# Ending layer norms in one VectorE pass, and moving small transfers of attention to another queue

## The chip, the cores and the metric

The kernel runs on one core of a Trainium2 chip. Times are device microseconds of the whole program; the time of a kernel is the median of several runs. The engines are TensorE (PE, with its weight loads PEld), VectorE (DVE), ScalarE (ACT), GpSimd (POOL) and SyncE (SP), which here only issues transfers (DMAs). Each engine works through its own list in order.

## The reference

Two layers of a decoder trunk, 1024 positions of width 1024 in float32. Layer 0 mixes tokens by dilated sliding-window attention, layer 1 by a gated linear recurrence; each mixer is followed by an MLP with squared ReLU (width 4096). After each of the four sub-layers:

```python
x <- layer_norm(alpha * x + sublayer(x), g, b)     # alpha = 4 ** 0.25

def layer_norm(x, g, b):
    mu = mean(x); var = mean((x - mu) ** 2)
    return (x - mu) * rsqrt(var + 1e-5) * g + b
```

Attention has three head groups with (window, dilation) = (128, 1), (512, 4), (2048, 16) and 16 heads of 64 columns each. A group gives, per position and head, an output and the logarithm of its softmax denominator (from the row maximum m and the sum l of exponentials); the three outputs are mixed with weights softmax(lse) over the groups, and the mix goes through the output matrix.

## The kernel before

Matrices are split in a high and a low part, and each product is three matmuls, so TensorE has most of the work. The input products of attention and the MLP's products follow a scheme that uses seven half-sized products in place of eight.

The work of attention is cut in 24 units: a pair of heads (8) by a group, in the order of dilation 16, 4, 1 within a pair. The units lie between the input products: `at(slot, f)` puts a step of a unit behind a certain product, with the slots written out by hand (`STATS`, `MIX`, `OFFS`). Through the body of attention the order of TensorE and VectorE is fixed as written (`in_order`); elsewhere, and on the other engines, a planner orders the instructions by the program's order and its own estimate of when they can start.

A unit's steps: `qk` (scores, with row maximum and exponential; the statistics go to `allS`), `ptr` and `pv` (transposed weights times values), then `combine_tr`: TensorE transposes `allS` (L566), ScalarE copies 32 rows of it to `sr` (L569), SP stores them in DRAM (L572) and loads them again into `ml` with a row for 16 (head, block) pairs (L578 for dilation 1, L581 for the others, where positions are regrouped). When a pair's third unit is through, `combine` works out the three factors per position on VectorE and ScalarE (L595 to L614), splits them in `fh` and `fl`, and SP copies six times two rows into the tile `frow` (L619). In `combine_mul` TensorE spreads a row of `frow` over the partitions (`fb`, L629) and VectorE multiplies the output with it (L630), adds the groups (L632, L633) and stores the mix.

The last two units don't fit between input products. Their steps stand in the hand-written list `mine` and are worked off by `tick` between the matmuls of the output product (`outproj_ln`: weights `wor`, activations `onr`, residual `z`, all by SP, with splits by ScalarE and VectorE at L137 and L138). The tail of attention is this stretch, from about 960 to 1062 us.

Every norm goes through `ln_math`, in place on a tile `z` of 128 positions by 1024 columns: statistics (L196, L198), `(z - mean) * g` in one VectorE pass (L199), the reciprocal root by ScalarE's logarithm and exponential with one step of refinement in small VectorE instructions (L204 to L206). The last eight of 32 norms, with `store`, end in two half passes on VectorE (L210). The other 24 end so:

```python
act(z, z, AF.Copy, scale=w[:, 3:4])      # L213, ScalarE
nc.gpsimd.tensor_add(z, z, bB)           # L214, GpSimd
```

Then `z` is stored for the next residual (L996, L1300) and transposed on TensorE (`lnpt`, L223), whose results are split by ScalarE and VectorE (L233, L234). In `outproj_ln` the calls `fin(t)` and `tr(t)` interleave products, norms and transposes of the eight tiles; L991 and L993 empty a product's PSUM bank (three banks `mm`) into `z`. In `ffn` norms are spread by `todo` between the steps of the second product.

Of the kernel before, what the change touches and what calls it, by code (L numbers as in the profile page):

```python
# [9 lines left out]
F32 = mybir.dt.float32  # L10
F32R = mybir.dt.float32r
U8 = mybir.dt.uint8
AF = mybir.ActivationFunctionType
ALU = mybir.AluOpType
AX = mybir.AxisListType

P = 128
# [5 lines left out]
DIL = (1, 4, 16)  # L23
# [39 lines left out]
def trunk_kernel(  # L63
# [24 lines left out]
    nc = tc.nc  # L88
# [7 lines left out]
    def U(name, dt=F32):  # L96
        return up.tile([P, 1024], dt, name=name, tag="u")

    def bank(tag, name):
        return ps.tile([P, 512], F32, name=name, tag=tag, bufs={"mm": 3, "s": 2, "pt": 2, "o": 1}[tag])  # L100

    def small(shape, name, bufs=4, dt=F32):
        return sp.tile(shape, dt, name=name, tag=name, bufs=bufs)

    act = nc.scalar.activation
# [87 lines left out]
    def ln_math(z, gB, bB, store=None):  # L193
        st = small([P, 2, 6], "lnst")
        for i in range(2):
            nc.vector.bn_stats(st[:, i], z[:, i * 512:(i + 1) * 512])  # L196
        mv = small([P, 2], "lnmv")
        nc.vector.bn_aggr(mv, st)  # L198
        nc.vector.scalar_tensor_tensor(z, z, mv[:, 0:1], gB, op0=ALU.subtract, op1=ALU.mult)  # L199
        w = small([P, 4], "lnw")  # L200
        act(w[:, 0:1], mv[:, 1:2], AF.Ln, bias=eps_ln)
        act(w[:, 1:2], w[:, 0:1], AF.Exp, scale=-0.5)
        r = w[:, 1:2]
        nc.vector.tensor_scalar(w[:, 2:3], mv[:, 1:2], LN_EPS, r, op0=ALU.add, op1=ALU.mult)  # L204
        nc.vector.tensor_scalar(w[:, 2:3], w[:, 2:3], r, -0.5, op0=ALU.mult, op1=ALU.mult)
        nc.vector.tensor_scalar(w[:, 3:4], w[:, 2:3], 1.5, r, op0=ALU.add, op1=ALU.mult)  # L206
        if store is not None:
            for i in range(2):
                c = slice(i * 512, i * 512 + 512)
                nc.vector.scalar_tensor_tensor(z[:, c], z[:, c], w[:, 3:4], bB[:, c], op0=ALU.mult, op1=ALU.add)  # L210
                nc.sync.dma_start(store[:, c], z[:, c])
            return
        act(z, z, AF.Copy, scale=w[:, 3:4])  # L213
        nc.gpsimd.tensor_add(z, z, bB)  # L214

    def z_tr(z):

# [104 lines left out]
    def attention(pre, hc):  # L322
# [121 lines left out]
        frow = U("frow", F32R)  # L444
# [19 lines left out]
        def nat(ap, g):  # L464
            d = DIL[g]
            return ap if d == 1 else ap.rearrange("p (n r) -> p n r", r=d)
# [97 lines left out]
        def combine_tr(pr, g, slot, ml):  # L564
            pt = bank("pt", "mpt")
            nc.tensor.transpose(pt[:, 0:P], allS, ident)  # L566
            q = slice(slot * 32, slot * 32 + 32)
            sr = small([P, P], "sr", 2)
            act(sr[q], pt[q, 0:P], AF.Copy)  # L569
            yield  # L570
            md = mdram[pr, g]
            nc.sync.dma_start(md.rearrange("w h (b q) -> (w h b) q", q=P), sr[q])  # L572
            yield

            d = DIL[g]
            for w in range(2):
                if d == 1:
                    nc.sync.dma_start(ml[:, w, 0, :], md[w].rearrange("h (i n) -> (h i) n", n=P))  # L578
                else:
                    for h in range(2):  # L580
                        nc.sync.dma_start(  # L581
                            ml[8 * h:8 * h + 8, w, g, :].rearrange("i (r n) -> i r n", r=d),
                            md[w, h].rearrange("(r i n) -> i r n", r=d, i=8))
            yield

        def combine(pr, ml):
            def cv(tl, g):
                d = DIL[g]
                return tl if d == 1 else tl.rearrange("p (r n) -> p n r", r=d)

            m = ml[:, 0]
            l = ml[:, 1]
            v = nc.vector
            mn = small([16, P], "mn", 1)
            v.tensor_tensor(nat(mn, 1), nat(m[:, 0], 1), cv(m[:, 1], 1), op=ALU.min)  # L595
            v.tensor_tensor(nat(mn, 2), nat(mn, 2), cv(m[:, 2], 2), op=ALU.min)
            for g in range(NG):
                v.tensor_sub(cv(m[:, g], g), nat(mn, g), cv(m[:, g], g))
            act(m, m, AF.Exp)
            yield  # L600
            v.tensor_mul(l, l, m)
            den = mn
            v.tensor_add(nat(den, 1), nat(l[:, 0], 1), cv(l[:, 1], 1))
            v.tensor_add(nat(den, 2), nat(den, 2), cv(l[:, 2], 2))
            yield
            v.reciprocal(den, den)
            for g in range(NG):
                v.tensor_mul(nat(l[:, g], g), cv(m[:, g], g), nat(den, g))

            fh = wp.tile([P, 512], F32R, name="fh", tag="p")[:16, :NG * P].rearrange("p (g t) -> p g t", t=P)  # L610
            fl = wp.tile([P, 512], F32R, name="fl", tag="pts")[:16, :NG * P].rearrange("p (g t) -> p g t", t=P)
            act(fh, l, AF.Copy)
            yield
            v.tensor_sub(fl, l, fh.bitcast(F32))  # L614
            yield
            for g in range(NG):
                for i, f in enumerate((fh, fl)):
                    r = 4 * g + 2 * i
                    nc.sync.dma_start(frow[r:r + 2, :].bitcast(F32).rearrange("h (i t) -> h i t", t=P),  # L619
                                      f[:, g, :].bitcast(F32))  # L620
            yield

        def combine_mul(pr, og, hb):
# [26 lines left out]
        ml, ogs = {}, {}  # L650
# [58 lines left out]
        def unit_work(gi, a, base):  # L709
# [20 lines left out]
            work = []  # L730
            later = [lambda: [f() for f in work.pop(0)] for _ in range(5)]
            trs = combine_tr(pr, g, slot, ml[pr])
            stats = [lambda: next(trs, None)] * 3
            mix = []
            if g == GORD[-1]:
                steps = combine(pr, ml[pr])
                mix = [lambda: next(steps, None)] * 5
                for hb in range(2):
                    muls = combine_mul(pr, ogs[pr], hb)
                    mix += [lambda muls=muls: next(muls, None)] * (4 + hb)  # L740
# [24 lines left out]
        for n in range(len(seq)):  # L765
            gi, i, j = seq[n]
# [26 lines left out]
            if n % 21 == 14:  # L793
# [27 lines left out]
        (ra, ca, sa, _), (rb, cb, sb_, mx) = tail  # L821
        done = [f for n in sorted(fill) for f in fill[n]]
        mine = [[ra[0]], [rb[0], rb[1]], [ra[1]], [ca[0], rb[2]], [ca[1]], [cb[0]], [ca[2]], [cb[1]], [ca[3]], [cb[2]],
                [ca[4]] + sa, [cb[3]], [ca[5]], [cb[4]] + sb_, [cb[5]], mx[:1], mx[1:3], mx[3:5], [],
                mx[5:7], mx[7:10], mx[10:]]
        lists = [done[k:k + 1] + (mine[k] if k < len(mine) else []) for k in range(max(len(done), len(mine)))]
        return oN, lists
# [62 lines left out]
    def outproj_ln(pr, oN, fill, resid, gB_ap, bB_ap, keep):  # L890
# [92 lines left out]
        def fin(t, dms=(0, 1)):  # L983
            load_z(t)
            for dm in dms:
                o = bank("mm", "pmm")
                c = slice(dm * 512, dm * 512 + 512)
                old = parts.get((t, dm), [])
                rows(o, a, w, t, dm, [k for k in range(NK) if k not in old], True, True)
                if old:  # L990
                    nc.vector.tensor_add(z[t][:, c], o, z[t][:, c])  # L991
                else:
                    nc.vector.scalar_tensor_tensor(z[t][:, c], z[t][:, c], ALPHA, o, op0=ALU.mult, op1=ALU.add)  # L993
            if 1 in dms:
                ln_math(z[t], gB, bB)
                nc.sync.dma_start(keep[t * P:(t + 1) * P, :], z[t])  # L996
# [22 lines left out]
    def ffn(li, xf, late, res, gB_ap, bB_ap, last, pre=None):  # L1019
# [275 lines left out]
        def norm_of(t):  # L1295
            if last:
                ln_math(z[t], norm["g"], norm["b"], out[t * P:(t + 1) * P, :])
                return
            ln_math(z[t], norm["g"], norm["b"])
            nc.sync.dma_start(x3d[t * P:(t + 1) * P, :], z[t])  # L1300
# [188 lines left out]
    def hgrn(xs, late, consts, pre, gw):  # L1489
# [104 lines left out]
        for hd in range(8):  # L1594
# [66 lines left out]
            if hd == 0:  # L1661
                new = [[]] + new
            pend = [(pend[i] if i < len(pend) else []) + (new[i] if i < len(new) else [])
                    for i in range(max(len(new), len(pend)))]
# [9 lines left out]
    pr = Out(w_attn_out, "a", 0)  # L1674
    hc = []
    oN, fill = attention(pr.pre_steps, hc)
    xf, late = outproj_ln(pr, oN, fill, lambda t: x[t * P:(t + 1) * P, :],
                          ln_mix_g[0], ln_mix_b[0], x1d)
# [85 lines left out]
```

## Time and profile before

| | us |
|---|---|
| median of 3 runs | 2829.61 (2828.23 to 2829.97) |
| profiled execution, its own time | 2828.98 |
| span of the profile | 2827.2 |
| TensorE busy / VectorE / ScalarE / GpSimd | 2766.7 / 2069.0 / 1450.8 / 122.9 |

The profile lists instructions by source line with engine, output and inputs, e.g. `L214 POOL TENSOR_TENSOR z<-z,bB`. In the timeline a row begins with its start and its duration; a bracket says how long the engine was idle before and what released it. A wait row reads "who waits <- for whom: us in total, times, longest". A group row of one source line gives the least, the median and the greatest duration in ns. "SPq" is SP's queue of transfers: its durations are those of issuing, not of the transfer. PEclk is the share of TensorE's full clock that was granted.

### The profile page before, as it was taken

The numbers are of one execution on the slowest core, as the hardware profiler recorded it, in microseconds if no ns is written. First come the engines' busy times: TensorE is split into PE (matmuls) and PEld (weight loads), VectorE is DVE, ScalarE is ACT, GpSimd is POOL, SyncE is SP. The second block draws the span as 40 slices with busy tenths as digits, with TensorE's granted clock in tenths as the row PEclk, the third lists the DMA queues.
The fourth block names the chain that finished last, engine by engine and source line by source line (L and its number), as shares of the span: only waits on it lengthen the run. The fifth ranks groups of instructions, "written<-read, shape, count | busy, mean of one in ns | idle before, by whom it ended". The sixth has DMA issues, their size and how long they took to land.

```text
span 2827.2 us, 40131 instructions
## 1 busy us (share of the span) xinstructions
PE 2766.7 (98%) x14280; PEld 2229.3 (79%) x14280; DVE 2069.0 (73%) x3830; ACT 1450.8 (51%) x3105; POOL 122.9 (4%) x68
## 2 busy tenths in 40 slices
PE   8999999999999989999999999999999999999998
PEld 6777777777777757888878887788887788878887
DVE  7768777777877767786686876565667787678687
ACT  5455555655555555544454444555553644454443
POOL 0000000000000003100000011111102200000000
PEclk9999999999999999999999999999999999999999
DMA  7766665766666523464494752011132355475654
GB/s 286 255 187 208 191 207 173 217 201 198 201 200 220 168 83 134 146 224 160 152 324 127 260 178 98 8 60 60 61 112 104 128 211 176 154 278 188 221 176 130
DMA packets 204936, 485.27 MB, mean 172 GB/s; under 512 B 29376, under 2 KB 43712, under 8 KB 204736
## 3 DMA queue, kind: packets, MB, share of 16 engines
q1 hardware_dynamic: 204736, 482.72, 51.1%
q8 instruction: 112, 1.84, 0.3%
q14 instruction: 88, 0.72, 0.1%
HBM read 362.82 MB, written 94.24 MB: 162 GB/s over the span
## 4 chain that ended last, share of the span: by engine, by line
PE 90%; DVE 5%; ACT 2%; DMA 1%; issue 1%; POOL 0%; SPq 0%; DVEq 0%; POOLq 0%; ACTq 0%
PE pmm L669 8%; PE pmm L671 8%; PE pmm L670 8%; PE pup L1118 7%; PE pup L1116 7%; PE pup L1117 7%; PE pdy L1268 4%; PE pdy L1264 4%; PE pdy L1267 4%; PE s L502 3%; PE pdx L1267 3%; PE pmm L171 3%; PE pdx L1268 3%; PE pmm L173 3%; PE pdx L1264 3%; PE pmm L172 3%
## 5 line engine op out<-in xcount | busy, mean ns | idle before, releaser
L669 PE MATMUL pmm<-xh,H 128*128 128x512 f32 x1008 | 408.5, 405 | 13.2 <-ACT H L432 9.6
L671 PE MATMUL pmm<-xh,H 128*128 128x512 f32 x1008 | 396.5, 393 | 0.2 <-DVE H L440 0.2
L670 PE MATMUL pmm<-xl,H 128*128 128x512 f32 x1008 | 396.0, 393 | 0.0
L669 PEld LDWEIGHTS pmm<-xh,H 128*128 128x128 f32 x1008 | 190.8, 189 | 54.1 <-ACT H L432 9.6
L671 PEld LDWEIGHTS pmm<-xh,H 128*128 128x128 f32 x1008 | 190.4, 189 | 42.6 <-DVE H L440 1.1
L670 PEld LDWEIGHTS pmm<-xl,H 128*128 128x128 f32 x1008 | 191.1, 190 | 36.6
L516 ACT ACTIVATE p<-p,stats 128x128 f32<-128x128 f32 (+1 forms) x384 | 168.3, 441 | 90.7 <-DVE stats L513 89.3
L1264 PE MATMUL pdy<-dT,dS 128*128 128x512 f32 x512 | 199.2, 389 | 0.0
L1267 PE MATMUL pdy<-dT,dS 128*128 128x512 f32 x512 | 199.2, 389 | 0.0
L1268 PE MATMUL pdy<-dT,dS 128*128 128x512 f32 x512 | 199.2, 389 | 0.0
L513 DVE CUSTOM_DVE_ANT_0 p<-s,mask 128x128 f32<-128x128 f32 (+1 forms) x384 | 113.3, 348 | 66.5 <-PE s L502 56.8
L137 ACT ACTIVATE dS<-dr 128x512 fp32r<-128x512 f32 x192 | 119.5, 622 | 73.1 <-PE pdy L1268 36.6
L171 PE MATMUL pmm<-f0nh,wh 128*128 128x512 f32 x384 | 153.1, 399 | 0.0
L173 PE MATMUL pmm<-f0nh,wl 128*128 128x512 f32 x384 | 150.1, 391 | 1.7 <-DVE wl L138 1.6
L172 PE MATMUL pmm<-f0nl,wh 128*128 128x512 f32 x384 | 149.8, 390 | 0.0
L138 DVE TENSOR_TENSOR dS<-dr,dS 128x512 fp32r<-128x512 f32 x192 | 135.4, 705 | 16.2 <-ACT dS L137 14.3
L214 POOL TENSOR_TENSOR z<-z,bB 128x1024 f32<-128x1024 f32 x24 | 58.6, 2444 | 1673.1 <-ACT z L213 1663.0
L529 ACT ACTIVATE pts<-ppt 128x256 f32<-128x256 f32 (+1 forms) x192 | 85.4, 474 | 61.1 <-PE ppt L526 59.0
L137 ACT ACTIVATE dT<-hold 128x512 fp32r<-128x512 f32 x128 | 80.0, 625 | 69.0 <-DVE hold L1243 28.4
L1077 ACT ACTIVATE H<-wc 128x512 fp32r<-128x512 f32 x128 | 77.2, 625 | 73.3 <-DVE wc L1070 43.9
L1267 PEld LDWEIGHTS pdy<-dT,dS 128*128 128x128 f32 x512 | 96.1, 188 | 20.0
L1268 PEld LDWEIGHTS pdy<-dT,dS 128*128 128x128 f32 x512 | 96.1, 188 | 20.0
(396 smaller groups left out, 6946.6 us busy)
## 6 DMA issues: line engine op xcount, KB each, us to landing
xh<-xtd SPq DMA_DIRECT2D x110, 512.0 KB
xl<-xtd SPq DMA_DIRECT2D x110, 512.0 KB
dr<-hd SPq DMA_DIRECT2D x192, 256.0 KB
dr<-in_w_down_dram SPq DMA_DIRECT2D x128, 256.0 KB
rot<-e SPq DMA_DIRECT2D x192, 128.0 KB
wa<-in_w_up_dram SPq DMA_DIRECT2D x48, 512.0 KB
wb<-in_w_attn_dram SPq DMA_DIRECT2D x36, 512.0 KB
wa<-in_w_attn_dram SPq DMA_DIRECT2D x33, 512.0 KB
```

The costliest lines, as they stand in the source:

```text
L137: act(hi, raw, AF.Copy)
L171: nc.tensor.matmul(o, wh[:, k], xs.h(k), start=k == 0, stop=False)
L172: nc.tensor.matmul(o, wh[:, k], xs.l(k), start=False, stop=False)
L173: nc.tensor.matmul(o, wl[:, k], xs.h(k), start=False, stop=k == NK - 1)
L669: nc.tensor.matmul(o, wh, hi[k // 2][:, c], start=begin and k == 0, stop=False, skip_group_check=True)
L670: nc.tensor.matmul(o, wh, lo[k // 2][:, c], start=False, stop=False, skip_group_check=True)
L671: nc.tensor.matmul(o, wl, hi[k // 2][:, c], start=False, stop=end and k == 3, skip_group_check=True)
L1116: nc.tensor.matmul(o, wh, xf.h(b, k), start=begin and k == 0, stop=False, skip_group_check=True)
L1117: nc.tensor.matmul(o, wh, xf.l(b, k), start=False, stop=False, skip_group_check=True)
L1264: nc.tensor.matmul(o[q], h, T_[:, L], start=begin, stop=False, skip_group_check=True)
L1267: nc.tensor.matmul(o[q], h, T_[:, R], start=False, stop=False, skip_group_check=True)
L1268: nc.tensor.matmul(o[q], l, T_[:, L], start=False, stop=end, skip_group_check=True)
```

## The change

`ln_math` without `store` ends in one VectorE instruction, z * factor + bias, in place of the ScalarE and the GpSimd instruction. In `combine_tr` the store of `sr` is issued by ScalarE; for dilation 1 there is no store and no load, but two copies from `sr` straight into `ml`, issued by ScalarE too. The loads for dilations 4 and 16 stay on SP. In `combine` the rows of `fh` are issued by ScalarE and those of `fl` by SP. In the list `mine` the first step of the statistics (transpose and copy) of the last unit moves ahead of the step `cb[4]`, the others ahead of `cb[5]`; for the unit before, the other steps move one place back.

```diff
-        act(z, z, AF.Copy, scale=w[:, 3:4])
-        nc.gpsimd.tensor_add(z, z, bB)
+        nc.vector.scalar_tensor_tensor(z, z, w[:, 3:4], bB, op0=ALU.mult, op1=ALU.add)
...
-            q = slice(slot * 32, slot * 32 + 32)
+            q0 = slot * 32
             sr = small([P, P], "sr", 2)
-            act(sr[q], pt[q, 0:P], AF.Copy)
+            act(sr[q0:q0 + 32], pt[q0:q0 + 32, 0:P], AF.Copy)
             yield
             md = mdram[pr, g]
-            nc.sync.dma_start(md.rearrange("w h (b q) -> (w h b) q", q=P), sr[q])
+            d = DIL[g]
+            if d == 1:
+                for w in range(2):
+                    nc.scalar.dma_start(ml[:, w, 0, :], sr[q0 + 16 * w:q0 + 16 * w + 16])
+            else:
+                nc.scalar.dma_start(md.rearrange("w h (b q) -> (w h b) q", q=P), sr[q0:q0 + 32])
             yield
-            d = DIL[g]
-            for w in range(2):
-                if d == 1:
-                    nc.sync.dma_start(ml[:, w, 0, :], md[w].rearrange("h (i n) -> (h i) n", n=P))
-                else:
+            if d > 1:
+                for w in range(2):
                     for h in range(2):
                         nc.sync.dma_start(
                             ml[8 * h:8 * h + 8, w, g, :].rearrange("i (r n) -> i r n", r=d),
...
-                for i, f in enumerate((fh, fl)):
+                for i, (f, eng) in enumerate(((fh, nc.scalar), (fl, nc.sync))):
                     r = 4 * g + 2 * i
-                    nc.sync.dma_start(frow[r:r + 2, :].bitcast(F32).rearrange("h (i t) -> h i t", t=P),
-                                      f[:, g, :].bitcast(F32))
+                    eng.dma_start(frow[r:r + 2, :].bitcast(F32).rearrange("h (i t) -> h i t", t=P),
+                                  f[:, g, :].bitcast(F32))
...
-                [ca[4]] + sa, [cb[3]], [ca[5]], [cb[4]] + sb_, [cb[5]], mx[:1], mx[1:3], mx[3:5], [],
+                [ca[4]] + sa[:1], sa[1:] + [cb[3]], [ca[5]], sb_[:1] + [cb[4]], sb_[1:] + [cb[5]], mx[:1], mx[1:3], mx[3:5], [],
```

## The prediction

> **What bounds the kernel now.** I read the page first: shares of busy time, then the chain that ended last.
>
> ```profile
> PE 2766.7 (98%) x14280; PEld 2229.3 (79%) x14280; DVE 2069.0 (73%) x3830; ACT 1450.8 (51%) x3105; POOL 122.9 (4%) x68
> ```
>
> ```profile
> PE 90%; DVE 5%; ACT 2%; DMA 1%; issue 1%; POOL 0%; SPq 0%; DVEq 0%; POOLq 0%; ACTq 0%
> ```
>
> TensorE works 98% of the span and carries 90% of the chain. The change takes nothing from TensorE, so only its idle time can be won, 60.5 us in all. Next the busy time by stretch: the body of attention, its tail, and three of the places where layer norms run.
>
> ```profile
> core 0: us, PE busy (x) PEld busy (x) DVE busy (x) ACT busy (x) POOL busy (x), PEclk, DMA share, GB/s
> 960.00:1062.00 102.00, 90.04 (x508) 64.16 (x507) 73.59 (x171) 49.25 (x135) 0.00 (x0) 0.97 0.31 97
> 1061.00:1096.00 35.00, 34.36 (x162) 27.82 (x161) 31.86 (x65) 15.79 (x35) 15.54 (x6) 1.00 0.19 76
> 1640.00:1680.00 40.00, 40.00 (x178) 33.14 (x177) 36.66 (x60) 20.22 (x40) 9.61 (x4) 1.00 0.45 144
> 1715.00:1755.00 40.00, 34.93 (x171) 28.16 (x170) 30.64 (x61) 20.27 (x48) 10.38 (x5) 1.00 0.35 126
> 2143.00:2182.00 39.00, 37.12 (x176) 30.39 (x175) 33.10 (x66) 15.33 (x34) 14.35 (x6) 1.00 0.17 68
> 125.00:940.00 815.00, 808.99 (x4788) 631.56 (x4784) 613.66 (x1348) 458.92 (x1245) 0.00 (x0) 1.00 0.64 200
> ```
>
> In the tail (960 to 1062) TensorE idles 12.0 us and its clock is below full; where the first MLP ends (1715 to 1755) it idles 5.1 us. In the two stretches behind the mixers' output products (1061, 2143) it idles 0.6 and 1.9 us, and there VectorE is busy 91% and 85%: a VectorE instruction added there may not be free. At 1640 TensorE has no idle time, in the body 6 us of 815. These are the stretches to price.
>
> **The layer norms.** Twenty-four of 32 norms end in a ScalarE pass and a GpSimd addition. Each gets one VectorE pass instead, of the same form as L199 (1024 wide, two operands in SBUF and a per-row factor).
>
> ```profile
> L213 ACT ACTIVATE z<-z,lnw x24: 1138/1152/1157, 1066.7 to 2202.5; 128x1024 f32<-128x1024 f32 x24
> L214 POOL TENSOR_TENSOR z<-z,bB x24: 2362/2396/3149, 1067.9 to 2203.7; 128x1024 f32<-128x1024 f32 x24
> L199 DVE SCALAR_TENSOR_TENSOR z<-z,lnmv,gB x32: 1265/1284/3417, 1063.8 to 2820.3; 128x1024 f32<-128x1024 f32 x32
> ```
>
> ScalarE loses 24 x 1.15 = 27.6 us, GpSimd 24 x 2.40 = 57.6 us, VectorE gains 24 x 1.28 = 30.8 us. One norm is ready 1.15 + 2.40 - 1.28 = 2.3 us sooner. But L199 once took 3.42 us instead of 1.28. That row, the GpSimd addition beside it and three like it, from the timeline; then all waits of TensorE from 1715 to 1755:
>
> ```profile
> 1067.95 2.40 POOL L214 TENSOR_TENSOR z<-z,bB 128x1024 f32<-128x1024 f32 x1 [967.54 <-ACT z L213]
> 1068.02 3.42 DVE L199 SCALAR_TENSOR_TENSOR z<-z,lnmv,gB 128x1024 f32<-128x1024 f32 x1
> 1724.82 2.56 DVE L138 TENSOR_TENSOR d3s<-d,d3s 128x256 fp32r<-128x256 f32 x1
> 1733.63 2.08 DVE L138 TENSOR_TENSOR d3s<-d,d3s 128x256 fp32r<-128x256 f32 x1
> 1748.56 2.50 DVE L138 TENSOR_TENSOR wl<-wr,wh 128x1024 fp32r<-128x1024 f32 x1 [2.23 <-ACT wh L137]
> ```
>
> ```profile
> PE lnpt L223 <- DVE f0nl L234: 2.1, 1, 2.1
> PE pmm L173 <- DVE wl L138: 1.6, 1, 1.6
> PE pdx L1268 <- DVE d3s L138: 1.2, 1, 1.2
> ```
>
> 1067.95 + 2.40 + 1.28 = 1071.6, and L199 ends at 1071.4: it does its work when the addition has ended. The three at 1724 to 1748 are the producers (or stand just ahead of the producer) that TensorE's three waits name: 2.1 + 1.6 + 1.2 = 4.9 us. Without L214 the blocks go. Two new passes then stand ahead of the d3s and f0nl instructions in VectorE's order; VectorE has 40.0 - 30.6 = 9.4 us idle in this stretch, so I leave 0.9 us of the wait. **Term B: -4.0 us**; ends -4.9 (all gone) and 0 (each pass of 1.28 us puts as much back as the block took).
>
> Behind attention's output product VectorE runs without a break from 1061 to 1086:
>
> ```profile
> 1079.00 0.22 DVE L206 TENSOR_SCALAR lnw<-lnw 128x1 f32<-128x1 f32 x1
> 1079.13 0.68 DVE L993 SCALAR_TENSOR_TENSOR z<-z,pmm 128x512 f32<-128x512 f32 x1
> 1080.61 0.48 PE L183 MATMUL pmm<-woh,aoh 128*128 128x512 f32 x1
> ```
>
> L993 empties the PSUM bank that the product at 1080.61 fills (three banks, two taken by the half tiles between), so the slack is 0.8 us. L206 at 1079.00 is the fourth norm's factor, and the new pass follows it directly. With four passes ahead L993 comes 4 x 1.28 = 5.1 us later, less the 2.1 us that L199 loses no more: 3.0 us, of which 0.8 is slack. **Term A: +2.2 us**; ends -0.5 (the 0.6 idle there goes, nothing new) and +4.3 (five passes less 2.1, all on the path). Behind the recurrence's product, two L199 and all of TensorE's waits from 2143 to 2182:
>
> ```profile
> 2168.31 2.65 DVE L199 SCALAR_TENSOR_TENSOR z<-z,lnmv,gB 128x1024 f32<-128x1024 f32 x1
> 2174.34 2.57 DVE L199 SCALAR_TENSOR_TENSOR z<-z,lnmv,gB 128x1024 f32<-128x1024 f32 x1
> ```
>
> ```profile
> PE lnpt L223 <- issue: 1.9, 2, 1.0
> ```
>
> VectorE's 39.0 - 33.1 = 5.9 us of idle time and the 2 x 1.3 us that these L199 get back take the six passes of 7.7 us in sum; but TensorE's two waits, for the banks of the transposes, hang on short VectorE instructions with a pass now between them: half a pass. **Term C: +0.7 us**; ends -1.9 (the idle time goes) and +2.6 (a whole pass at each wait). The eight tiles outside these stretches: four run beside the MLP's second product, at 1640, where TensorE never idles; four beside its first, whose weights are split ahead. I cost them at nothing; without that cover each costs a pass, 1.3 us.
>
> **Attention's statistics.** Per unit, a store of `sr` and two or four loads of `ml` on SP's queue; per pair, six factor rows. These rows have the cost of issuing:
>
> ```profile
> L572 SPq DMA_DIRECT2D mdram<-sr x24: 317/328/338, 125.2 to 1033.5; - x24
> L619 SPq DMA_DIRECT2D frow<-fh x24: 610/623/712, 242.7 to 1049.2; - x24
> ```
>
> ScalarE gets 16 stores, 16 direct copies and 24 factor rows: 16 x 0.33, 16 x 0.40 (two loads of `ml` take 0.80 us in a row below) and 24 x 0.62, 26.6 us in all; SP loses those and eight more stores. Behind an issue on ScalarE stand its exponentials and copies, and TensorE waits for those. In the body ScalarE is idle 44%; a triple of rows (1.9 us) comes eight times. **Term D: +0.5 us**; ends 0 and +5, a third of each triple on the path. SP's waits for `sr` turn, for dilations 4 and 16, into a wait of the load for the store's landing; ahead of it weights and activations now go out earlier, so this costs TensorE nothing unless a load for the next slot stands behind it (in D's upper end).
>
> In the tail I read SP's queue at two places, one wait of TensorE, and the last pair's chain:
>
> ```profile
> 979.93 0.68 SPq L619 DMA_DIRECT2D frow<-fh  x1
> 980.71 0.35 SPq L911 DMA_DIRECT2D z<-in_x_dram  x1
> ```
>
> ```profile
> 1033.53 0.33 SPq L572 DMA_DIRECT2D mdram<-sr  x1
> 1033.90 0.90 SPq L864 DMA_DIRECT2D wor<-in_w_attn_out_dram  x2
> 1034.97 0.80 SPq L578 DMA_DIRECT2D ml<-mdram  x2
> 1035.82 0.42 SPq L875 DMA_DIRECT2D onr<-ond  x1
> ```
>
> ```profile
> PE pmm L183 <- DVE z L937: 1.5, 1, 1.5
> ```
>
> ```profile
> 1038.67 0.36 DVE L595 TENSOR_TENSOR mn<-ml 16x128 f32<-16x128 f32 x1
> 1041.47 0.74 PE L183 MATMUL pmm<-woh,aoh 128*128 128x512 f32 x1 [3.62 <-ACT aoh L137]
> 1045.75 0.62 SPq L619 DMA_DIRECT2D frow<-fh  x1
> 1049.85 0.61 SPq L619 DMA_DIRECT2D frow<-fl  x1
> 1051.98 0.77 PE L629 MATMUL fb<-frow,bsel 128*128 128x512 f32 x1 [2.46 <-DMA frow<-fh]
> ```
>
> SP stands for `fh` until 979.93, and the residual `z` behind it costs TensorE 1.5 us (its wait for L937): gone. The store at 1033.53 holds back weights `wor` and activations `onr`; ScalarE's splits wait for them and TensorE 3.6 us for ScalarE: mostly gone. But TensorE can't finish before the last pair's chain: statistics, `mn`, factors, rows, `fb`. That moves by 1.5 (TensorE arrives earlier), by 1034.97 - 1033.53 = 1.4 at `mn` (no hop by DRAM) and by 3 x 0.62 = 1.9 at the rows (from two queues), 4.8 in all, and 0.2 more because the first `fb` products run below the full clock now (0.97 over the stretch). The reordered hand list puts the last transpose of statistics a step earlier and its copy at about the old place, in line with this. **Term T: -5.0 us**; ends -1.9 (only the rows) and -9 (most of the idle 12.0).
>
> On the two queues: the six rows take 4.7 us to issue and the first product waits 2.46 us, so issuing is most of it. The Trainium skill ("DMA: Bandwidth & Descriptors", "Issuing engines are not separate DMA queues") says that a second issuing engine saves only the issue time, usually small beside the transfer; in these rows it isn't small. If it were small here, 1.9 us of T would fail and the sum be 2825.3.
>
> **Sum.** B -4.0, A +2.2, C +0.7, D +0.5, T -5.0: -5.6 us on the profiled execution's 2828.98 us (span 2827.2 and 1.8 around it) gives 2823.4 us. That execution is 0.6 below the median 2829.61 of the runs, so against the median it is -6.2, 0.22%. About 0.2% (5.7 us) is what a measurement of this kernel tells from no change: the forecast lies near that border.
>
> **Rivals.** *The tail's wait only moves* (chance 0.22): SP now waits at the factor rows' low half and at the loads for the stores to land, and `z`, `wor` and `onr` come no earlier. T is then -1.9 and the time 2826.5, no change. For it: SP's order still holds those rows ahead of later loads. Against it: the store that held them is off the queue.
>
> *VectorE becomes the bound in the norms* (0.16): A +4.3, C +2.6, B 0; with D and T 2828.98 + 2.4 = 2831.4, no change or a touch slower. For it: 91% busy at 1061. Against it: the blocked instructions quoted, which free VectorE as well.
>
> *ScalarE's issues reach TensorE* (0.12, the other side): ScalarE works its list in order, so 26.6 us of issues stand ahead of exponentials. With the other terms at -6.1, it turns slower than the median by over 0.2% when more than 6.1 + 0.6 + 5.7 = 12.4 us, some 47%, arrive; at 60% (16.0) the time is 2838.9. For it: the 3.62 us in the tail are a wait for ScalarE. Against it: ScalarE's 44% idle share in the body.
>
> The forecast keeps 0.50, of which 0.05 at its border is no change. Faster by over 0.2%: 0.45; within: 0.05 + 0.22 + 0.13 = 0.40; slower: 0.12 + 0.03 of the second rival = 0.15. Range 2816.0 to 2832.0: below, T at -9 and B at -4.9 with A small; above, the second rival; it leaves out most of the last. The likeliest case's own range is 2818 to 2825.
>
> **What would show it.** B: no VectorE instruction over its median at 1720 to 1750, TensorE idle there under 2 us. A: TensorE waits for L993 near 1081 by some 2 us. C: waits before the transposes of about a microsecond remain. D: TensorE's idle time in the body stays near 6 us. T: `z` and `wor` are issued before `sr` is ready, and the last `frow` is issued some 5 us earlier. I am wrong if TensorE's idle time in the body grows by several us, or the tail still idles 12 us.

## The result, and the profile after

The changed kernel takes 2818.42 us, the median of 7 runs (2816.95 to 2824.02); the kernel before took 2828.24 in its 7. The ratio is 0.9964, 95% interval 0.9955 to 0.9974: 10 us faster, 0.36%. The forecast was 2823.4, range 2816 to 2832. The direction and the range held; the sum was 5 us too high, and not for one reason: two terms had the wrong sign and a third was far too large.

The page of the changed kernel, busy time by engine:

```profile
PE 2767.4 (98%) x14280; PEld 2231.8 (79%) x14280; DVE 2070.8 (73%) x3854; ACT 1425.6 (51%) x3081; POOL 64.5 (2%) x44
```

VectorE has 24 instructions more, some 30.7 us of work, and is busy 1.8 us longer. That line holds the main lesson of this case: the additions on GpSimd had cost VectorE most of what the pass that replaced them costs.

The profiled execution is the slowest of the seven, 5.6 us above their median. The reason is one transfer in the body (its timeline, VectorE and TensorE):

```profile
757.74 1.23 DVE L474 TENSOR_TENSOR rot<-rot,sinT 128x1024 f32<-128x1024 f32 x1 [8.73 <-DMA rot<-e]
760.88 0.50 PE L672 MATMUL pmm<-xh,H 128*128 128x512 f32 x1 [2.96 <-DVE H L439]
```

A rotation's transfer landed some 3 us late, and TensorE waited 2.96 us. To see whether the change does that, the same kernel ran once more:

> The changed kernel once more. In its first profile VectorE stood 8.7 us for a rotation's transfer at 749 to 757.7 (5.6 us in the profile of before) and TensorE 2.96 us behind it, with a half clock after. Theory 1 (chance of that one execution): neither is there now, and the time of the profiled execution is within 2 us of the median, 2818.4. Rival (it is the change: something on ScalarE's queue delays that transfer each time): the 2.96 us are there again.

It took 2818.70 (5 runs; ratio 0.9965, 0.9952 to 0.9979), and TensorE has no wait there. So it was that execution, and from here the second profile stands for the changed kernel. Its stretches, with the bounds used in the prediction:

```profile
core 0: us, PE busy (x) PEld busy (x) DVE busy (x) ACT busy (x) POOL busy (x), PEclk, DMA share, GB/s
125.00:940.00 815.00, 809.16 (x4797) 632.19 (x4794) 613.64 (x1348) 458.39 (x1245) 0.00 (x0) 1.00 0.65 200
960.00:1062.00 102.00, 92.49 (x514) 66.63 (x513) 74.22 (x171) 49.35 (x134) 0.00 (x0) 0.93 0.31 95
1061.00:1096.00 35.00, 35.00 (x167) 28.98 (x167) 33.24 (x68) 8.46 (x26) 0.00 (x0) 1.00 0.23 89
1715.00:1755.00 40.00, 38.57 (x191) 32.12 (x190) 30.38 (x63) 18.03 (x43) 0.00 (x0) 1.00 0.43 158
2143.00:2182.00 39.00, 39.00 (x188) 31.99 (x187) 35.28 (x70) 12.35 (x34) 0.00 (x0) 1.00 0.39 148
```

TensorE no longer idles behind the two output products (0.6 and 1.9 us before); where the first MLP ends 1.4 us are left of 5.1. In the tail it idles 9.5 us instead of 12.0, but its clock there fell from 0.97 to 0.93.

To place the gains, the timelines of all profiles were cut at the same five waits of TensorE (near 118, 969, 1424, 1791 and 2093) and at the first wait near 2511: at the end of the first of these waits, at the start of the others. Only four stages differ between kernels; the one from 1791 to 2093 took 302.5 us in every kernel of the table, the last, up to TensorE's last matmul, 307.4 to 307.5. In us:

| kernel (median of its runs) | attention's body | tail, norms, first product | end of first MLP | second product, second MLP |
|---|---|---|---|---|
| before (2828.24) | 850.5 | 454.9 | 366.6 | 417.8 |
| changed, first profile (2818.42) | 854.7 | 452.0 | 362.0 | 417.0 |
| changed, again (2818.70) | 849.9 | 452.5 | 362.0 | 415.4 |
| norms alone (2820.91) | 849.7 | 453.3 | 362.0 | 416.6 |
| attention alone (2826.77) | 849.9 | 454.2 | 366.4 | 417.6 |
| VectorE addition (2819.61) | 849.9 | 452.6 | 362.0 | 416.9 |
| GpSimd times one (2826.56) | 850.2 | 453.6 | 368.6 | 415.4 |
| two ScalarE copies (2829.41) | 849.9 | 458.4 | 362.7 | 420.2 |
| extra VectorE pass (2837.67) | 848.9 | 461.2 | 364.8 | 423.3 |
| one queue for rows (2821.53) | 851.5 | 454.4 | 362.0 | 416.3 |
| norms and rows (2817.80) | 851.9 | 450.8 | 362.0 | 416.1 |

These are single executions. The body varies by some 2 us (more in the first profile, with its late transfer), and the last column by 1.6 in one and the same kernel (a wait of 0.8 us near 2337 that comes in some); the two in the middle are steadier.

### The profile page after: what moved, and what is told of

Read it like the earlier page. It is cut to its first block, busy times and chain, and to the rows that moved or that the text cites. A ratio compares the mean times of both kernels' runs of the same rounds, so it can differ in the third digit from the quotient of the medians.

```text
span 2822.2 us, 39965 instructions
## 1 busy us (share of the span) xinstructions
PE 2767.4 (98%) x14280; PEld 2231.8 (79%) x14280; DVE 2070.8 (73%) x3854; ACT 1425.6 (51%) x3081; POOL 64.5 (2%) x44
## 3 DMA queue, kind: packets, MB, share of 16 engines
q10 hardware_dynamic: 1712, 0.59, 0.1%
## 5 line engine op out<-in xcount | busy, mean ns | idle before, releaser
L1265 PEld LDWEIGHTS pdy<-dT,dS 128*128 128x128 f32 x512 | 96.1, 188 | 20.0
L1268 PEld LDWEIGHTS pdy<-dT,dS 128*128 128x128 f32 x512 | 96.1, 188 | 20.0
L1269 PEld LDWEIGHTS pdy<-dT,dS 128*128 128x128 f32 x512 | 96.1, 188 | 19.9
```

What stands on the lines that cost most here:

```text
L1265: nc.tensor.matmul(o[q], h, T_[:, L], start=begin, stop=False, skip_group_check=True)
L1268: nc.tensor.matmul(o[q], h, T_[:, R], start=False, stop=False, skip_group_check=True)
L1269: nc.tensor.matmul(o[q], l, T_[:, L], start=False, stop=end, skip_group_check=True)
```

## The experiments: the norms

**The two parts alone.** Norms alone: the kernel before with the new end of `ln_math`. Attention alone: everything else of the change.

> Only the layer norms' end is changed; attention's transfers and the hand list stay as before. Theory 1 (GpSimd's additions blocked VectorE, and VectorE has room for the passes): TensorE's waits of 4.9 us at 1715 to 1755 and of 1.9 us at 2143 to 2182 go and nothing new comes behind attention's output product, so 6 to 8 us faster than before (about 2821). Theory 2 (the prediction's terms: B -4.0, A +2.2, C +0.7): 1.1 us faster, not to be told from no change. Rival (the norms gave nothing, the gain is all attention's): 0, and the waits at 1715 stay.

> Only attention's transfers and the hand list are changed; the norms end as before. Theory 1 (from the two traces: the tail gained about 3 us and ScalarE's issues cost nothing): 2 to 3 us faster than before. Theory 2 (the prediction's D +0.5 and T -5.0): 4.5 us faster. Rival (the tail's wait only moves and the 26.6 us of issues reach TensorE in the body): 0 to 3 us slower.

Norms alone: 2820.91, ratio 0.9970 (0.9959 to 0.9982), 7.8 us faster than the 2828.75 of before in the same comparison. Attention alone: 2826.77, ratio 0.9992 (0.9983 to 1.0001), 2.0 us faster and hardly to be told from no change. They add up to the whole. By the table the norms gain 1.7 us (before rounding) in the column of attention's product, 4.6 where the first MLP ends and 1.2 to 2.4 in the last column. The page of norms alone, and its VectorE rows at the place that the prediction feared, the fourth norm behind attention's product:

```profile
PE 2765.7 (98%) x14280; PEld 2229.3 (79%) x14280; DVE 2074.2 (74%) x3854; ACT 1426.6 (51%) x3081; POOL 64.5 (2%) x44
```

```profile
1076.78 1.27 DVE L213 SCALAR_TENSOR_TENSOR z<-z,lnw,bB 128x1024 f32<-128x1024 f32 x1
1077.96 0.20 DVE L198 BATCH_NORM_AGGREGATE lnmv<-lnst 128x2 f32<-128x12 f32 x1
1078.08 0.64 DVE L992 SCALAR_TENSOR_TENSOR z<-z,pmm 128x512 f32<-128x512 f32 x1
1078.63 1.28 DVE L199 SCALAR_TENSOR_TENSOR z<-z,lnmv,gB 128x1024 f32<-128x1024 f32 x1
```

VectorE's busy time grew by 5.2 us for 30.7 us of passes, so 25.5 us came back. Counted instruction by instruction, against the median of the same operation on the same tiles (where it is over by more than 0.1 us), VectorE's time over the median fell from 59.3 to 38.7 us, so 20.6 us of it is blocked time seen in the rows (23.0 in the changed kernel's second profile). And L992 (L993 before), which empties the bank, now starts at 1078.08, before the fourth norm's L199; in the kernel before it came behind L199 and the three factor instructions, at 1079.13. The planner had reordered the queue.

**Is it the block, the shorter chain, or ScalarE's pass?** Three kernels start from the changed one and put one suspect back; the planner orders each anew. Behind `bB`'s pass, or in its place:

```diff
 (VectorE addition)
-        nc.vector.scalar_tensor_tensor(z, z, w[:, 3:4], bB, op0=ALU.mult, op1=ALU.add)
+        act(z, z, AF.Copy, scale=w[:, 3:4])
+        nc.vector.tensor_add(z, z, bB)
 (GpSimd times one)
+        nc.gpsimd.tensor_mul(z, z, one.broadcast_to([P, D]))
 (two ScalarE copies)
+        act(z, z, AF.Copy)
+        act(z, z, AF.Copy)
```

> The changed kernel, but each of the 24 norms ends in the ScalarE pass of before (z times the factor, 1.15 us) and an addition of the bias on VectorE: no GpSimd, the same VectorE time, ScalarE's pass back in its order. Theory 1 (all the gain of the norms is that GpSimd's block is gone): within 1 us of the changed kernel's 2818.6. Theory 2 (where the first MLP ends it is the block; behind the two output products it is ScalarE's pass, which stands in ScalarE's order ahead of the copies that free the banks of the transposes; two ScalarE copies cost 5.9 and 4.7 us there): the 4.6 us at 1715 to 1755 stay, the 1.7 and 2.4 us behind the products go, about 2822.5.

2819.61, ratio 0.9969 (0.9958 to 0.9980): within 1 us of the changed kernel, as theory 1 says. By the table ScalarE's pass costs nothing in the first three columns. Behind the recurrence's product it does: the last column is 416.9 where the changed kernel's second profile has 415.4, and TensorE has a wait there (2138 to 2178) that the changed kernel does not have:

```profile
PE pmm L183 <- DVE z L995: 1.1, 1, 1.1
```

So theory 2 fails behind attention's product, and behind the recurrence's this one profile bears it out in part.

> The changed kernel; behind each of the 24 norms' last VectorE pass GpSimd multiplies z by one (two operands, in place), so that GpSimd's pass is back, beside the VectorE passes, and a norm is ready some 2.4 us later. Theory 1 (GpSimd's two-operand pass blocks VectorE): VectorE passes of 2.5 to 3.4 us come back, TensorE's waits at 1715 to 1755 and 2143 to 2182 too; 6 to 9 us slower than the changed kernel's 2818.6, about 2826. Rival (VectorE isn't blocked, only the shorter chain counted): no long VectorE passes, and the time is that of the run with two ScalarE copies.

2826.56, ratio 0.9994 (0.9985 to 1.0003): the time is back where it was, though not place by place. GpSimd's pass takes 1.89 us here (the addition took 2.40). Page, then GpSimd and VectorE at the end of the first MLP, then TensorE's waits there (1712 to 1752):

```profile
PE 2768.9 (98%) x14280; PEld 2232.4 (79%) x14280; DVE 2085.4 (74%) x3854; ACT 1425.5 (50%) x3081; POOL 118.4 (4%) x68
```

```profile
1734.26 1.89 POOL L214 TENSOR_TENSOR z<-z,one 128x1024 f32<-128x1024 f32 x1 [5.34 <-DVE z L213]
```

```profile
1734.04 0.42 DVE L234 TENSOR_TENSOR f0nl<-lnpt,f0nh 128x256 fp32r<-128x256 f32 x1
1734.37 2.06 DVE L138 TENSOR_TENSOR d3s<-d,d3s 128x256 fp32r<-128x256 f32 x1
1736.35 0.74 DVE L234 TENSOR_TENSOR f0nl<-lnpt,f0nh 128x256 fp32r<-128x256 f32 x2
```

```profile
PE lnpt L223 <- DVE f0nl L234: 4.8, 2, 3.5
```

The d3s instruction has both operands in SBUF; it takes 2.06 us beside GpSimd's pass and 0.41 without. L234 has one operand in PSUM (`lnpt`) and runs at its usual 0.42 while the pass at 1734.26 has begun; three more of it lie wholly within the pass at 1750.99 (2.81 us), 0.42 each. Behind the blocked instruction wait the copies that free a transpose's bank, and TensorE 3.5 us for them. That costs 6.6 us in this stage: TensorE waits 4.8 us where the changed kernel waits 1.4, and the rest comes with 6.8 us at half clock from 1735.9, which the kernel before did not have. It can also go the other way round. At 1675 VectorE began first, 0.15 us ahead, with a row of instructions whose operands are both in SBUF; they keep their time, and GpSimd's pass takes 6.30 us:

```profile
1675.42 6.30 POOL L214 TENSOR_TENSOR z<-z,one 128x1024 f32<-128x1024 f32 x1 [5.86 <-DVE z L213]
1675.87 0.41 DVE L138 TENSOR_TENSOR d3s<-d,d3s 128x256 fp32r<-128x256 f32 x1
```

The Trainium skill states the same ("SBUF — State Buffer", "Who interferes with whom"): a VectorE instruction with two SBUF inputs contends with a GpSimd instruction that reads SBUF, and which of the two blocks is decided by the order of issue; this trace agrees (2.06 against 0.41 us, 0.42 with one input in PSUM, and the pass of 6.30 us where VectorE began first).

Behind the recurrence's product TensorE has no wait in this kernel (2143 to 2187): there GpSimd's pass brought nothing back, against the expectation.

> The changed kernel; behind each of the 24 norms' last VectorE pass ScalarE copies z onto itself twice (2 x 1.15 us), so that a norm is ready as late as before the change, without GpSimd. Theory 1 (blocking): 0 to 2 us slower than the changed kernel's 2818.6. Rival (the gain of the norms, 7.8 us, is the 2.3 us by which a norm is ready sooner): 6 to 9 us slower.

2829.41, ratio 1.0003 (0.9994 to 1.0012): 10.7 us slower than the changed kernel. At first sight that speaks for the rival. For one stage the table says otherwise: at the first MLP's end, where GpSimd's pass cost 6.6 us, the same delay without GpSimd costs 0.7; the loss lies in the two other columns, 5.9 and 4.7 us, where GpSimd's pass, with nearly the same delay, cost 1.1 and nothing. The waits of TensorE and of ScalarE from 1100 on:

```profile
PE lnpt L224 <- DVE fs L302: 4.1, 1, 4.1
```

```profile
ACT z L214 <- DVE z L213: 4.3, 2, 4.1
```

ScalarE stands 4.1 us at the copy for VectorE's pass, with everything behind it in its order held up. But that copy need not be the cause: the kernel with an extra VectorE pass (the next experiment) has no such copy, and TensorE waits at the same transpose, from 1100 to 1135:

```profile
PE lnpt L226 <- DVE fs L304: 4.3, 1, 4.3
```

In both kernels TensorE's list has a transpose at that place where the changed kernel's has the next product. The order that the planner wrote is a likely cause, and it was not tested. The expectation for the block, 0 to 2 us, holds only in the stage of the first MLP's end.

So the block is shown as the cause where the first MLP ends (4.6 us): GpSimd's pass brings the wait back, ScalarE's two copies hardly do. Behind the two output products it is not. GpSimd's pass put back costs 1.1 us in the column of attention's product and nothing behind the recurrence's; a norm that is ready later, and ScalarE's pass itself, are not ruled out there.

**Is a VectorE pass free?**

```diff
+        for i in range(2):
+            nc.vector.bn_stats(spare[:, i], z[:, i * 512:(i + 1) * 512])
```

> The changed kernel with one more pass of VectorE behind each of the 24 norms: statistics of z's two halves into a spare tile that nobody reads, some 1.28 us, so 30.7 us in all. VectorE is busy 34.09 of 35 us from 1061 to 1096 in the changed kernel, 36.3 of 39 from 2138 to 2177, 33.4 of 39 from 1712 to 1751. Theory 1 (a pass is free up to VectorE's idle time of its stretch and costs in full beyond it): 5 passes less 0.9 us behind attention's product and 6 less 2.7 behind the recurrence's, 5.5 + 5.0, about 10 us slower than 2818.6. Theory 2 (the prediction's rule: the half of a pass at a wait, and what passes the slack of 0.8 us at the bank): 4.3 + 1.3 + 0.9, some 6.5 us slower. Rival (VectorE is not near its limit): within 2 us.

2837.67, ratio 1.0032 (1.0019 to 1.0045): 19 us slower than the changed kernel, for 24 passes. Page and three stretches (each five or six norms):

```profile
PE 2771.7 (98%) x14280; PEld 2235.5 (79%) x14280; DVE 2100.5 (74%) x3902; ACT 1425.7 (50%) x3081; POOL 63.9 (2%) x44
```

```profile
1055.00:1090.00 35.00, 34.62 (x159) 28.50 (x158) 35.00 (x68) 5.32 (x18) 0.00 (x0) 0.99 0.18 76
1713.00:1753.00 40.00, 37.77 (x179) 30.84 (x178) 35.60 (x76) 15.85 (x45) 0.00 (x0) 0.96 0.30 108
2145.00:2184.00 39.00, 37.83 (x173) 30.97 (x173) 38.28 (x73) 6.43 (x21) 0.00 (x0) 1.00 0.17 68
```

VectorE's busy time grew by 28.8 us against the 2071.7 of the changed kernel's second profile, and the kernel is 19 us slower, nearly twice the largest expectation. VectorE is busy without a break behind attention's product. But not all of this is VectorE at its limit. In its profile, compared with the changed kernel's second one matmul by matmul, 3.7 us are lost behind attention's product, 2.8 where the first MLP ends and 3.1 behind the recurrence's. Another 10.0 us come at the transposes that follow the two products, near 1128 and 2220: two waits of TensorE of 4.3 us (the first is shown above) and half clock after them. No expectation had these; for the places that they priced, theory 1 was not too low but too high (5.5 and 5.0 us against 3.7 and 3.1). So the fear behind terms A and C was right about a pass; it was wrong about the sum, because the norms' new end added 3 to 5 us of VectorE's busy time, not 31.

## The experiments: attention's tail

**Rows on one queue again, and rows alone.** First the changed kernel with `fh` and `fl` both issued by SP; then norms alone with the rows from two queues and nothing else of attention's part:

```diff
 (one queue, against the changed kernel)
-                for i, (f, eng) in enumerate(((fh, nc.scalar), (fl, nc.sync))):
+                for i, (f, eng) in enumerate(((fh, nc.sync), (fl, nc.sync))):
 (norms and rows, against norms alone)
-                for i, f in enumerate((fh, fl)):
+                for i, (f, eng) in enumerate(((fh, nc.scalar), (fl, nc.sync))):
```

> The changed kernel with all six factor rows of a pair issued by SP, as before the change. Theory 1 (in the changed kernel TensorE doesn't wait for the rows but for VectorE's splits and products): within 1 us of 2818.6. Prediction's term (the rows stand on the path, 3 x 0.62 us): 1.9 us slower, with a wait of TensorE for frow of about 2 us. Rival (24 issues less on ScalarE): 1 us faster.

2821.53, ratio 0.9974 (0.9964 to 0.9984), 2.8 us slower than the changed kernel. But TensorE has no wait for `frow` in the tail: what came back is the earlier one, for the residual `z`. SP's queue and that wait:

```profile
980.22 0.68 SPq L620 DMA_DIRECT2D frow<-fh  x1
981.00 1.32 SPq L912 DMA_DIRECT2D z<-in_x_dram  x3
```

```profile
PE pmm L183 <- DVE z L938: 1.7, 1, 1.7
```

SP stands for `fh` with three residuals behind it. With the high rows on ScalarE they go out ahead of that.

> The kernel before with two parts of the change alone: the norms' end, and the factor rows from two queues. The store of the statistics, the loads for dilation 1 and the hand list are as before the change, so that VectorE does the last pair's statistics one behind the other again. Theory 1 (of attention's part only the rows earn anything: putting them back on one queue cost 2.9 us, all of attention's part is worth 2.0): the norms' 2820.9 less 2.9, about 2818, as fast as the changed kernel (2818.6) or up to 1 us faster. Theory 2 (the prediction's terms: the store off SP's queue and the statistics on chip are worth 1.5 + 1.4 us of the tail): 2 to 3 us slower than the changed kernel, about 2821.

2817.80, ratio 0.9960 (0.9946 to 0.9973): at least as fast as the whole change. Its SP row, and TensorE's waits in the tail (960 to 1062):

```profile
976.55 1.32 SPq L910 DMA_DIRECT2D z<-in_x_dram  x3
```

```profile
PE pmm L183 <- ACT aoh L137: 4.7, 2, 3.9
PE fb L628 <- DMA frow<-fl: 0.6, 1, 0.6
```

`z` is out some 4.5 us sooner than on one queue, and the wait for the rows is 0.6 us where it was 2.46 before the change. The rows alone bring the norms' 2820.91 down by 3.1 us; so the store on ScalarE, the statistics on chip and the new list together bring nothing; whether they cost a microsecond (2818.70 against 2817.80) these intervals do not tell. They were not run one by one.

**Why the other parts brought nothing.** VectorE, ScalarE and TensorE's first wait in the tail of the changed kernel (second profile):

```profile
1033.33 0.39 DVE L596 TENSOR_TENSOR mn<-ml 16x128 f32<-16x128 f32 x1 [1.08 <-DMA wor<-in_w_attn_out_dram]
1033.65 0.67 DVE L633 TENSOR_TENSOR og<-og 128x512 f32<-128x512 f32 x1
1034.25 0.67 DVE L138 TENSOR_TENSOR aol<-onr,aoh 128x512 fp32r<-128x512 f32 x1
1034.85 0.67 DVE L631 TENSOR_TENSOR og<-og,fb 128x512 f32<-128x512 f32 x1
1035.45 0.37 DVE L597 TENSOR_TENSOR mn<-mn,ml 16x128 f32<-16x128 f32 x1
...
1038.04 0.37 DVE L599 TENSOR_TENSOR ml<-mn,ml 16x128 f32<-16x128 f32 x1
```

```profile
1038.45 0.52 ACT L600 ACTIVATE ml<-ml 16x384 f32<-16x384 f32 x1 [3.01 <-DVE ml L599]
1039.40 0.61 ACT L137 ACTIVATE aoh<-og 128x512 fp32r<-128x512 f32 x1
1043.18 0.52 ACT L613 ACTIVATE fh<-ml 16x384 fp32r<-16x384 f32 x1 [2.65 <-DVE ml L609]
```

```profile
PE pmm L183 <- ACT aoh L137: 4.6, 1, 4.6
```

From `mn` to `fh` the last pair took 1045.20 - 1038.67 = 6.5 us before and takes 1043.18 - 1033.33 = 9.9 us now: the planner, given other arrival times, puts products and splits of 0.7 us between the statistics' instructions. ScalarE stands 3.0 us at the exponential, and the split that TensorE waits for stands behind it. In the kernel with norms and rows alone `mn` to `fh` is 1044.22 - 1037.71 = 6.5 us. Two kernels tried to mend the order:

> The changed kernel, but in the tail ScalarE's exponential of the last pair's statistics stands behind two splits of activations, not ahead of them (order fixed by a dependency; the hand list gives the combine steps later). In the changed kernel ScalarE stands 2.69 us at that exponential for VectorE, and the split that TensorE waits 4.13 us for stands behind it. Theory 1 (head of line on ScalarE): that wait falls to 1 to 2 us, one half-clock window goes, and the time is 2 to 4 us below the changed kernel's (about 2815). Rival (the last pair's factor rows set the end of the tail anyway): TensorE waits as much longer for frow, and the time is the same as the changed kernel's within 1 us.

> The changed kernel with another order in attention's tail: the second half of the last but one pair's mix (five VectorE instructions of 0.6 us that only the second half of the rows needs) goes behind the last pair's statistics, its first half is handed on as soon as it is mixed, and the exponential stands behind ScalarE's split. In the changed kernel these five stand between the statistics' VectorE instructions and hold back the splits that TensorE waits 4.4 us for, with the clock halved for 10.2 us after. Theory 1 (VectorE's order in the tail is the limit): TensorE's wait falls below 2.5 us, the half-clock time to 3.4 or 6.8 us, and the time is 3 to 6 us below the changed kernel's 2818.6. Rival (the last pair's chain from statistics to factor rows ends the tail in any order): the wait turns up at frow, and the gain is below 1 us.

The first gave 2818.11 (ratio 0.9958, 0.9945 to 0.9970), no change: the split did come first, but TensorE then stood 4.4 us for the low half on VectorE. The second gave 2824.07 (ratio 0.9983, 0.9974 to 0.9991), 5.5 us slower: the first statistics instructions now stand one behind the other, but the later ones have other work between them (`mn` to `fh` takes 11.6 us), the deferred products hold up a broadcast, and a later wait for a split takes the place of the first. TensorE's waits in the tail, of the first kernel and of the second:

```profile
PE pmm L187 <- DVE aol L140: 4.6, 2, 4.4
```

```profile
PE pmm L190 <- ACT aoh L144: 3.6, 1, 3.6
PE fb L640 <- DVE og L641: 2.6, 2, 2.2
```

So the wait at the head of ScalarE's queue is not the limit by itself, and neither edit bettered the order on VectorE: that VectorE's order is the limit of the tail fits these rows, but no run that mends it shows it.

**The clock.** The granted clock over three pieces of the tail, changed kernel, second profile:

```profile
1038.20:1048.40 10.20, 7.61 (x17) 5.54 (x18) 6.73 (x14) 3.75 (x7) 0.00 (x0) 0.50 0.04 11
1048.50:1055.20 6.70, 4.65 (x17) 2.77 (x16) 4.65 (x8) 1.26 (x2) 0.00 (x0) 1.00 0.81 261
1055.30:1058.70 3.40, 3.40 (x9) 2.42 (x8) 3.37 (x7) 0.63 (x1) 0.00 (x0) 0.50 0.00 0
```

The clock was halved for 10.2 and 3.4 us; before the change it was two times 3.4. The last experiment gives TensorE 16 matmuls without use during its wait:

```diff
+            for i in range(16):
+                nc.tensor.matmul(o, a[0][0](0), w[0][0][:, 0:512], start=True, stop=True)
```

> The changed kernel; ahead of the matmul that waits 4.1 to 4.6 us near 1036, TensorE does 16 matmuls on operands that are there, into a bank that nobody reads (16 x 0.227 = 3.6 us). Theory 1 (the gap brings the half clock: 10.2 us at 0.5 cost 5.1 us, and 3.4 us more of half clock than before the change took the gain of the tail): no half clock at 1038 to 1048, and 3 to 5 us faster than 2818.6, about 2814.5. Rival (the half clock is hidden, since TensorE would wait for the last pair's rows or for VectorE anyway): the time between 0.5 us faster and 1 us slower.

2815.85, ratio 0.9956 (0.9943 to 0.9968), the lowest median of all, 2.8 us under the changed kernel's. TensorE's wait fell to 1.5 us and the long half-clock piece went, but a piece of 6.8 us now came at 1048 behind a wait for the rows, and in this profile the tail stage is only 0.7 us shorter (451.9). Its body has no half clock at 119 us, which is worth some 1.5 us and lies 900 us ahead of the edit. The gain in the median is therefore not explained by more than 0.7 us, and its interval overlaps the changed kernel's.

## Why the prediction was right or wrong

Against the profile of before the second profile of the changed kernel is 10.3 us shorter (the medians 9.8), where the terms said 5.6.

- **B (-4.0): right.** The stage became 4.6 us shorter, 1.4 us of the waits are left (0.9 forecast). The long VectorE instructions are gone, and GpSimd's pass alone brings some of them back, and the wait.
- **A (+2.2): wrong sign, -1.7.** Two steps failed. "The new pass follows it directly", so that L993 comes behind four passes: the queue was taken as fixed, and the planner put it behind three and ahead of the fourth L199, so that it starts 1.0 us sooner (1078.08 for 1079.13) and not 3.0 later. And only one blocked instruction was credited (2.1 us); a second in the same stretch, an L199 of 2.25 us at 1088.05, was not read, while over the kernel 20.6 us of the 30.7 us of passes came out of blocked time. How much of the 1.7 belongs to each is open.
- **C (+0.7): wrong sign, -2.4** (1.2 in the profile of norms alone, which has the wait near 2337). The two blocked L199 were read and priced; but they were set against VectorE's idle time, with half a pass left at each wait. And the two waits were put down to short VectorE instructions. What TensorE's transposes waited for was a copy on ScalarE, L291, which empties their bank; it ended 0.1 us before, both times, and stood right behind ScalarE's pass L213, which the change takes away:

```profile
2172.18 1.14 ACT L213 ACTIVATE z<-z,lnw 128x1024 f32<-128x1024 f32 x1
2173.22 0.59 ACT L291 ACTIVATE hf11r<-lnpt 128x512 f32<-128x512 f32 x1
2173.91 1.10 PE L223 MATMUL lnpt<-ident,z 128*128 128x128 f32 x8 [0.90 <-issue]
```

The blocked L199 at 2168.31 (1.3 us too long) stood ahead in that chain as well. Either would do for a wait of 0.9 us: with ScalarE's pass alone put back, or GpSimd's alone, these two waits stay away. Which of the two the gain is due to is not separated.
- **D (+0.5): about right.** TensorE idles 5.8 us in the body (6.0 before); 26.6 us of issues on ScalarE do not show. The rival that ended slower finds nothing for it.
- **T (-5.0): far too large, -0.7** (454.9 to 454.2 with attention's part alone; up to the product near 1062 it is -1.3, and 0.5 is lost behind it; the waits fell by more, but the clock took it back). The 1.5 us for `z` came, though from the rows that left SP, not from the store. The 1.9 us for the rows came at their wait: with the norms and the rows alone it is 0.6, but only 0.9 us of that reaches the end of the tail. The wait of 3.6 us for ScalarE's split, forecast as "mostly gone", is 4.6 now. The 1.4 us of the hop by DRAM reached `mn` and were lost in VectorE's order, and the 0.2 us for the clock had the wrong sign: half-clock time went from 6.8 to 13.6 us. The Trainium skill's rule ("DMA: Bandwidth & Descriptors", "Issuing engines are not separate DMA queues"), that a second issuing engine saves only issue time, usually small, would have made the rows worth little; putting them back on one queue cost 2.8 us, of which TensorE's wait for `z`, which stood behind them in the queue, is 1.7.

Of the rivals, "the tail's wait only moves" (0.22) describes T best: its -1.9 is nearer than -5.0. Had A and C come as forecast, it would have been the result. "VectorE becomes the bound" was wrong about the change; one pass more comes nearer to it.

The terms that failed lie on both sides (A and C 7.0 us too high, T 4.3 too low), so the sum came nearer than its parts by luck.

## What to carry to other kernels

When a GpSimd instruction is removed, add up what VectorE lost beside it over the whole kernel, instruction by instruction against the median of its form, before pricing the VectorE instruction that takes its place; here two thirds of the new passes came back that way, and VectorE's busy time grew by 2 to 5 us for 30.7 us of passes. A transfer's price on a queue is what stands behind it, not its own issue time. And where a planner orders the instructions, a chain that begins sooner may end later: ask which order it will write, not only which wait goes.

## What was unexpected of the hardware

The half clock comes in pieces of 3.4 us or twice or three times that. Every profile has a wait of 2.09 us near 117 us; in 10 of 14 the clock is then halved for 3.4 us, in 4 it is not. Where no other wait in the body differs, the body without it takes 848.3 and 848.4 us and with it 849.9 in four profiles, 848.9 in a fifth, so about 1.5 us. Such a chance may be part of the spread between runs of one kernel: of 27 runs of the kernel before, the 15 with a granted clock of 0.995 took 2829.0 us in the mean, the 5 with 0.997 or 0.998 2827.2. The Trainium skill ("TensorE: Matmul & The Clock Gate", "HAM oscillation — how this bites in real kernels") gives as the rule no idle gaps of TensorE above some 3.4 us; in these profiles a half clock followed a gap of 2.09 us more often than not.

A second thing is that the block between GpSimd and VectorE costs either side: the same GpSimd pass took 1.89 us beside a VectorE instruction that it held up for 1.6 us, and 6.30 us where VectorE's instructions had begun first.
